# Splitting the next group's rows earlier, and moving two steps of the recurrence, in a one-core hybrid layer

## Chip, cores and metric

The kernel runs on one core of a Trainium2 chip. The metric is device time in microseconds (us); less is better. One compiled program computes the whole layer, and its inputs and outputs lie in HBM.

## What is computed

A layer of a streaming encoder over 2048 positions of width 1024, float32 throughout. The parts that the change touches, cut from the reference:

```python
h = rms_norm(x, mix_norm_g[i])
z = h @ w_in[i]                        # 1024 -> 3328 columns
y_conv = short_conv_mixer(z_conv, conv_mix_w[i])       # B * conv3(C * x_in)
y_rwkv = rwkv7_mixer(z_rwkv, ...)      # g = sigmoid(gd) @ g_up ; o = wkv7_scan(...) ; o * g
x = x + concatenate([y_conv, y_rwkv], axis=-1) @ w_out[i]
x = x + conv_glu_ffn(rms_norm(x, ffn_norm_g[i]), ...)  # 1024 -> 5632 -> 1024
e = rms_norm(p[i] @ ple_w_proj[i], ple_norm_g[i])
gate = sigmoid(rms_norm(x, ple_gate_norm_g[i]) @ ple_w_gate[i])
x = x + gate * e
return rms_norm(x, final_norm_g)
```

wkv7_scan is a recurrence over positions in 8 heads of 64. The kernel does it in chunks of 64 positions, with a triangular solve in each chunk.

## The kernel before

Positions are cut into 4 groups of 512. Activations lie transposed, 128 channels by 512 positions in a tile, which is called a row here (8 rows for width 1024). A float32 product is made of three faster ones: each operand is split into a high part in the float32r type (hi) and a remainder (lo), and `mm3` issues hi*hi, hi*lo and lo*hi. Weights are split in the first group that uses them (ScalarE copy, GpSimd subtraction, line 154), written to HBM as split pairs (SP's queue, line 175) and read from there by the later groups (GpSimd's queue, line 165). The ring of weight halves has four places, that is two products.

**Two streams share TensorE.** The dense stream is a generator. First `all_in` runs the input projection of all four groups, 26 products each. Then, for each group, `dense_rest` runs the output projection (8 products), the up and down projections of the feed-forward part, a small embedding product, and the gate product (8 products). A product is 24 matmuls of 128x128 by 512; it yields in the middle and at its end. The side stream `rwkv` is the recurrence: 16 units of 128 positions, each a generator of 41 steps. `drive` takes a step of the side stream for each step of the dense one (0.85 of a step in the output and gate projections). The side stream begins in the second half of the first input group, and ends in the third group's gate projection. `rest(n)` lets n steps pass; R_LM, R_LOAD, R_DN and so on are such counts.

**Order on the engines.** Each engine runs its instructions in one fixed order. Matmuls keep the order in which they are written, and so do instructions marked with `pin`. All others are placed by a planner that simulates the program before it is compiled; `high_priority` moves them ahead.

**Rows.** `Rows.add` squares a row for the norm (`SumSq.add`: ScalarE L233, VectorE add L237) and splits it with its gain (`split_g`: ScalarE L218, VectorE L221). The norm's factor is applied behind the product: the first two products of a projection are held (HELD = 2) until the sum of squares is complete. Rows y, the input of the output projection, are the mixers' outputs; they come from HBM, have no norm, and are split by `residual` (ScalarE copy L155, pinned; GpSimd subtraction L158). Rows 0 to 3 of y are written by the short convolution during the input projection, rows 4 to 7 by the units of the recurrence. `in_next(g)` and `out_next(g)` load row k and split row k - 1 at call k. Loads share a ring of four buffers, the split halves a ring of 32, which is two sets of eight rows.

**A unit of the recurrence**, as far as it matters here: step 1 ps_s, ps_a; step 2 ps_n, ps_v; step 3 ps_l twice, then ps_g (the gate-lora product) and its copy. Later the score products and the matrix lt, which goes through HBM (ld on ScalarE's queue, lm on SP's) and comes back in another layout. R_LM steps later `fold` starts the triangular solve on VectorE: three instructions and 16 pairs of a multiply (L828) and a reduction (L832). The result goes through HBM again (xd, dt on SP's queue); the next unit's rows are loaded behind it. R_LOAD steps later `rwkv_first` prepares the next unit; R_DN steps later `dn` transposes dt, pinned on VectorE; the rest of the 20 steps (WAIT) pass, and the products gm_ps and x_ps use dn. Seven of these PSUM tiles a unit, and eight others, come from one pool of three buffers.

Of the kernel before, what the change touches and what calls it, by code (L numbers as in the profile page):

```python
# [9 lines left out]
F32 = mybir.dt.float32  # L10
# [6 lines left out]
P = 128  # L17
G = 512
KD = 8
# [1 line left out]
PLE_AT = 2  # L21
HELD = 2
WAIT = 20
R_LM = 4
R_DN = 7
R_POST = 3
R_LOAD = 6
# [37 lines left out]
def tile_trunk(  # L65
# [18 lines left out]
    nc = tc.nc  # L84
    T = xT.shape[2]

    def matmul(*args, **kw):
        return pin(nc.tensor.matmul(*args, **kw))  # L88
# [4 lines left out]
    def pin(ins):  # L93
        return tc.keep_in_program_order(ins)

    NG = T // G
# [25 lines left out]
    def v(name, i, n=1):  # L122
        o, _ = VEC[name]
        return vec[:, o + i : o + i + n]
# [56 lines left out]
    def weight(pools, src, name):  # L181
        return [
            half(pools, src[:, 512 * c : 512 * c + 512], f"{name}_{c}", f"{name}_{c}")
            for c in range(2)
        ]
# [13 lines left out]
    def blk(k):  # L199
        return slice(k * P, (k + 1) * P)  # L200

    def buf(pools, name):
        return pools["tmp"].tile([P, G], F32, tag="b", name=name, bufs=NBUF)
# [6 lines left out]
    def slot(pools, name):  # L210
        return pools["act"].tile([P, G], F32R, tag="act", name=name)

    def pair(pools):
        return slot(pools, "hi"), slot(pools, "lo")

    def split_g(pools, src, gcol, dst, late=False):
        hi, lo = dst
        ins = nc.scalar.activation(hi, src, AF.Copy, scale=gcol)  # L218
        if late:
            pin(ins)  # L220
        nc.vector.scalar_tensor_tensor(  # L221
            out=lo, in0=src, scalar=gcol, in1=hi.bitcast(F32), op0=ALU.mult, op1=ALU.subtract
        )
        return dst
# [43 lines left out]
    class Rows:  # L268
# [1 line left out]
            self.hs, self.ss, self.scale, self.held = [], SumSq(), None, []  # L270

        def add(self, pools, x, gcol, late=False):
            self.ss.add(pools, x, late)
            with tc.high_priority():
                self.hs.append(split_g(pools, x, gcol, pair(pools), late))

    def product(pools, w, rows, evac):
        ps = pools["psd"].tile([P, G], F32, tag="d", name="ps_mm")
# [26 lines left out]
    def in_proj(pools, g, rows, nxt):  # L305
        def project(m, evac):
            return product(pools, weight(pools, w_in[m], f"in{m}"), rows, evac)

        def lerp(j):
            def evac(ps, rstd):  # L310
                zb = scaled(pools, ps, rstd, z_last[:, j : j + 1], 1)
                u = buf(pools, "u")
                nc.scalar.activation(u, zb[:, 2 : G + 2], AF.Copy, scale=mu_c[:, j : j + 1])
                nc.vector.scalar_tensor_tensor(
                    out=u, in0=zb[:, 1 : G + 1], scalar=v("rwkv_mu", j), in1=u,
                    op0=ALU.mult, op1=ALU.add,
                )
                nc.scalar.dma_start(out=zs[g][:, j, :], in_=u)
            return evac

        for j in (12, 0, 4, 8, 13, 1, 5, 9, 2, 6, 10, 3, 7, 11):
            yield from project(12 + j, lerp(j))

        for i in range(4):
            st = {}

            def evac_x(ps, rstd):
                x = st["x"] = buf(pools, "xin")
                nc.vector.tensor_tensor(out=x, in0=ps, in1=rstd, op=ALU.mult)
                nc.vector.tensor_tensor(out=x, in0=x, in1=rstd, op=ALU.mult)  # L330

            def evac_c(ps, rstd):
                t = scaled(pools, ps, st["x"], cx_last[:, i, :], 2)
                u = st["c"] = buf(pools, "cu")
                nc.scalar.activation(u, t[:, 2 : G + 2], AF.Copy, scale=v("conv_mix_w", 8 + i))
                for d in (1, 0):
                    nc.vector.scalar_tensor_tensor(
                        out=u, in0=t[:, d : d + G], scalar=v("conv_mix_w", 4 * d + i), in1=u,
                        op0=ALU.mult, op1=ALU.add,
                    )  # L340

            def evac_b(ps, rstd):
                u = buf(pools, "yc")
                nc.vector.tensor_tensor(out=u, in0=ps, in1=rstd, op=ALU.mult)
                nc.vector.tensor_tensor(out=u, in0=u, in1=st["c"], op=ALU.mult)
                nc.scalar.dma_start(out=ys[g][:, i, :], in_=u)

            if i:
                nxt(3 * i - 3)
            yield from project(i, evac_x)  # L350
            if i:
                nxt(3 * i - 2)
            yield from project(8 + i, evac_c)
            if i:
                nxt(3 * i - 1)
            yield from project(4 + i, evac_b)

    def ple_load(pools, g):
# [44 lines left out]
    def dense_rest(pools, g, yrows, nxt):  # L403
# [3 lines left out]
        rows = Rows()  # L407
# [94 lines left out]
        def e_load(m):  # L502
            with tc.high_priority():
                return staged(pools, es[g][:, m, :], "e")

        ahead = e_load(0)
        for m in range(KD):
            nxt(m)
            w = weight(pools, w_gate[m], f"g{m}")
            e = ahead  # L510
            with tc.high_priority():
                nc.vector.tensor_tensor(out=e, in0=e, in1=re, op=ALU.mult)

            def evac(ps, rstd, m=m, e=e):
                th = buf(pools, "gt")
                nc.vector.tensor_tensor(out=th, in0=ps, in1=rstd, op=ALU.mult)
                if m:
                    ss.add(pools, x2[m - 1])
                nc.scalar.activation(th, th, AF.Tanh, scale=0.5)
                nc.vector.scalar_tensor_tensor(  # L520
                    out=th, in0=th, scalar=1.0, in1=e, op0=ALU.add, op1=ALU.mult
                )
                nc.vector.scalar_tensor_tensor(
                    out=x2[m], in0=th, scalar=pg_h[:, m : m + 1], in1=x2[m],
                    op0=ALU.mult, op1=ALU.add,
                )
                if m == KD - 1:
                    ss.add(pools, x2[m])

            steps = product(pools, w, rows3, evac)  # L530
            next(steps)
            yield SLOW
            if m + 1 < KD:
                ahead = e_load(m + 1)
            for _ in steps:
                yield SLOW
        nxt(KD)

        def finish():
            rstd = ss.rstd(pools)  # L540
# [69 lines left out]
    def rwkv_unit(rp, S, u, loaded, following):  # L610
        pr, ch, ps_p, ps_c = rp["prep"], rp["chain"], rp["ps_p"], rp["ps_c"]
        g, off = u // 4, (u % 4) * P
# [3 lines left out]
        def big(name, tag="t", pool=rp["t"]):  # L616
            return pool.tile([P, 4, P], F32, tag=tag, name=f"{name}{u}")
# [23 lines left out]
        r_t, k_t, v_t, gd, kr, sq = loaded  # L641
# [8 lines left out]
            matmul(ps[:, ct, :], S["aup"][:, blk(ct)], ad, start=True, stop=True)  # L650
        tha = big("tha")
        nc.scalar.activation(tha, ps, AF.Tanh, scale=0.5)
        yield

        ps_n = ps_p.tile([P, G], F32, tag="p", name="ps_n")
# [42 lines left out]
        for cp in range(2):  # L698
            ps = ps_p.tile([P, G], F32, tag="p", name="ps_l")
            for c in range(2):  # L700
                matmul(
                    ps[:, c * 130 : c * 130 + 130], sg[:, blk(2 * cp + c)], tri[:, 0:130],
                    start=True, stop=True,
# [1 line left out]
            pv = ps[:, 0:260].rearrange("p (a c i) -> p a c i", a=2, c=2)  # L705
            nc.scalar.activation(ep[:, 2 * cp : 2 * cp + 2], pv, AF.Exp, scale=-DECAY)
            nc.scalar.activation(em[:, 2 * cp : 2 * cp + 2], pv, AF.Exp, scale=DECAY)
        ps_g = ps_p.tile([P, 4, P], F32, tag="p", name="ps_g")
        for ct in range(4):
            matmul(ps_g[:, ct, :], S["gup"][:, blk(ct)], gd, start=True, stop=True)  # L710
        g_t = big("g")
        nc.scalar.copy(g_t, ps_g)
        yield
        yield

# [90 lines left out]
        for r in range(4):  # L806
# [4 lines left out]
            )  # L811
        yield from rest(R_LM)
        lmf = lm.rearrange("p i j -> p (i j)")
# [48 lines left out]
        for pq in range(4):  # L862
            q = pq % 2
            rs = slice(32 * pq, 32 * pq + 32)
            pin(nc.gpsimd.tensor_copy(tT[rs, :, :, 32 * q : 32 * q + 32], dt4[rs]))
        yield from rest(WAIT - R_LM - R_LOAD - R_DN)
        gm_ps = ps_c.tile([P, 8, 32], F32, tag="c", name="gm_ps")
        for n in range(8):
            c, ct = n // 4, n % 4
# [101 lines left out]
    pools, rp = {}, {}  # L971
# [13 lines left out]
    S = rwkv_setup(rp)  # L985
# [13 lines left out]
    rows = {(kind, g): Rows() for kind in ("in", "out") for g in range(NG)}  # L999
# [2 lines left out]

    def in_next(g):
        def run(k):
            if g < NG:
                if k < KD:
                    loads["in", g, k] = in_load(pools, g, k)
                if k:
                    in_row(pools, rows["in", g], k - 1, loads.pop(("in", g, k - 1)), g > 0)
        return run  # L1010

    def out_next(g):
        def run(k):
            if g < NG:
                if k < KD:
                    while k >= 4 and marks["done"] < 4 * g + 3:
                        next(side, None)
                    loads["out", g, k] = out_load(pools, g, k)
                if k:
                    out_row(pools, rows["out", g], k - 1, loads.pop(("out", g, k - 1)))  # L1020
        return run
# [10 lines left out]

    def all_in():
        for g in range(NG):
            yield from in_proj(pools, g, rows["in", g], in_next(g + 1))

    for k in range(KD + 1):
        in_next(0)(k)
# [7 lines left out]
            ):  # L1046
                tc.keep_in_program_order(nc.scalar.dma_start(out=dst, in_=src))
    drive(stream)
    for k in range(KD + 1):
        out_next(0)(k)  # L1050
    for g in range(NG):
        drive(dense_rest(pools, g, rows["out", g], out_next(g + 1)))
# [69 lines left out]
```

## Time and profile before

| | |
|---|---|
| median of 3 runs | 2913.43 us (2905.58 to 2913.78) |
| profiled execution | 2908.33 us, span of the instructions 2906.6 us |
| mean granted TensorE clock | 0.981 of full speed |
| TensorE (PE) busy | 2767.7 us, 95% |
| VectorE (DVE) busy | 1921.2 us, 66% |
| GpSimd (POOL) busy | 1106.0 us, 38% |
| ScalarE (ACT) busy | 961.6 us, 33% |
| HBM traffic | 216 GB/s over the span |

PE is TensorE's matmuls, PEld its weight loads, which overlap them; SP is the engine that issues DMAs. The profiled execution is one run of its own; its span is the time from the first to the last instruction. A line number (L88) is the line in the kernel; helpers that issue for many callers have one line, so the tile's name tells the instructions apart (ps_mm is a product's sum, whlo the split weights of the output projection, whlu, whld and whlg those of up, down and gate). An arrow points from what an instruction waits for to what it writes: `hi<-y` writes hi from y.

### The profile page before, as it was taken

How to read it: one execution, taken by the hardware profiler on the slowest of the kernel's cores; microseconds unless marked ns; L12 is line 12 of the kernel's file. 1: busy time of each engine (PE TensorE's matmuls, PEld its weight loads, DVE VectorE, ACT ScalarE, POOL GpSimd, SP SyncE). 2: the span in 40 equal slices, each digit the busy share in tenths (PEclk: the TensorE clock that was granted, in tenths of full speed). 3: DMA queues.
4: the chain of work that ended last, by engine and by line, in shares of the span. 5: the costliest groups of instructions: out<-in, count | busy, mean ns of one | idle time of the engine just before them, and what ended most of it. 6: DMA issues, size and time to landing. Idle time of an engine off the chain costs nothing.

```text
span 2906.6 us, 42088 instructions
## 1 busy us (share of the span) xinstructions
PE 2767.7 (95%) x15464; PEld 2228.2 (77%) x15464; DVE 1921.2 (66%) x3039; ACT 961.6 (33%) x1721; POOL 1106.0 (38%) x1700
## 2 busy tenths in 40 slices
PE   8989999998999999889999999899999999999997
PEld 6778778886777867667778887678788877788885
DVE  4575656646788777786876677777676865544446
ACT  4432231313453334343512123434122233411114
POOL 4532232324556556452433333333333332433321
PEclk9999999999999999999999999999999999999998
DMA  9886767777777767667665665777566668766665
GB/s 321 297 268 205 232 206 227 215 213 231 247 262 261 242 241 248 221 221 241 212 182 170 187 185 167 216 218 215 171 185 179 180 183 261 223 193 191 191 193 166
DMA packets 285801, 629.94 MB, mean 217 GB/s; under 512 B 60186, under 2 KB 113690, under 8 KB 285596
## 3 DMA queue, kind: packets, MB, share of 16 engines
q0 software_dynamic: 95040, 346.07, 39.7%
q1 hardware_dynamic: 144384, 238.08, 24.6%
q10 hardware_dynamic: 46172, 43.11, 4.5%
q8 instruction: 122, 2.00, 0.3%
q14 instruction: 83, 0.68, 0.1%
HBM read 467.77 MB, written 159.38 MB: 216 GB/s over the span
## 4 chain that ended last, share of the span: by engine, by line
PE 60%; DVE 19%; DMA 8%; issue 7%; ACT 3%; POOL 2%; SPq 1%; ACTq 0%; DVEq 0%; POOLq 0%
PE ps_mm L88 40%; PE ps_d L88 12%; DVE uf L433 3%; DVE pd L828 2%; PE ps_e L88 2%; DVE xs L832 1%; DMA lm<-ld 1%; PE o_ps L88 1%; DVE zb L263 1%; DMA whlo<-ko 1%; DMA ld<-ltt 1%; DMA whld<-kd 1%; PE s_ps L88 1%; PE u_ps L88 1%; DVE sq L237 1%
## 5 line engine op out<-in xcount | busy, mean ns | idle before, releaser
L88 PE MATMUL ps_mm<-hi,whlu 128*128 128x512 f32 x2816 | 905.5, 396 | 3.4 <-POOL whlu L158 2.3
L88 PEld LDWEIGHTS ps_mm<-hi,whlu 128*128 128x128 f32 x2816 | 531.1, 189 | 119.8 <-POOL whlu L158 3.9
L88 PE MATMUL ps_mm<-hi,whlin 128*128 128x512 f32 x1664 | 540.6, 399 | 16.9 <-DVE xs L832 8.1
L88 PE MATMUL ps_mm<-lo,whlu 128*128 128x512 f32 x1408 | 550.7, 391 | 0.4 <-DVE lo L221 0.4
L88 PE MATMUL ps_d<-hi,whld 128*128 128x512 f32 x1408 | 462.6, 401 | 20.6 <-DVE x L473 8.3
L88 PEld LDWEIGHTS ps_mm<-hi,whlin 128*128 128x128 f32 x1664 | 316.3, 190 | 88.0 <-DVE xs L832 8.9
L433 DVE SCALAR_TENSOR_TENSOR uf<-zb,vec,uf 128x512 f32<-128x512 f32 x352 | 305.7, 870 | 108.8 <-ACT uf L428 97.5
L88 PEld LDWEIGHTS ps_d<-hi,whld 128*128 128x128 f32 x1408 | 269.4, 192 | 85.6 <-DVE x L473 11.2
L88 PE MATMUL ps_mm<-lo,whlin 128*128 128x512 f32 x832 | 328.5, 395 | 2.4 <-DVE lo L221 2.4
L88 PEld LDWEIGHTS ps_mm<-lo,whlu 128*128 128x128 f32 x1408 | 266.2, 189 | 55.8 <-issue 1.9
L428 ACT ACTIVATE uf<-zb,vec 128x512 f32<-128x512 f32 x176 | 143.1, 815 | 493.5 <-DVE zb L263 491.9
L165 POOL DMA_DIRECT2D whlu<-ku x264 | 142.2, 539 | 426.1 <-PE ps_mm L88 281.6
L263 DVE TENSOR_TENSOR zb<-ps_mm,rstd 128x512 f32<-128x512 f32 x216 | 148.6, 688 | 207.1 <-PE ps_mm L88 204.8
L88 PE MATMUL ps_d<-lo,whld 128*128 128x512 f32 x704 | 278.5, 396 | 0.0
L473 DVE TENSOR_TENSOR x<-ps_d,x 128x512 f32<-128x512 f32 x192 | 131.1, 686 | 144.5 <-PE ps_d L88 144.2
L165 POOL DMA_DIRECT2D whlin<-kin x156 | 84.2, 540 | 277.5 <-PE ps_mm L88 243.5
L88 PE MATMUL ps_mm<-hi,whlo 128*128 128x512 f32 x512 | 169.9, 408 | 20.0 <-ACT hi L155 18.2
L88 PEld LDWEIGHTS ps_mm<-lo,whlin 128*128 128x128 f32 x832 | 158.2, 190 | 37.5 <-DVE lo L221 6.2
L88 PE MATMUL ps_mm<-hi,whlg 128*128 128x512 f32 x512 | 166.3, 399 | 2.0 <-DMA whlg<-kg 2.0
L233 ACT ACTIVATE sq<-x 128x512 f32<-128x512 f32 x128 | 80.6, 630 | 255.4 <-DVE x L411 73.6
L158 POOL TENSOR_TENSOR lo<-th,hi 128x512 fp32r<-128x512 f32 x88 | 117.0, 1330 | 113.8 <-ACT hi L155 113.6
L88 PEld LDWEIGHTS ps_d<-lo,whld 128*128 128x128 f32 x704 | 135.2, 192 | 26.7
(205 smaller groups left out, 4266.9 us busy)
## 6 DMA issues: line engine op xcount, KB each, us to landing
whlu<-ku POOLq DMA_DIRECT2D x264, 512.0 KB, 4.4
whlin<-kin POOLq DMA_DIRECT2D x156, 512.0 KB, 4.6
whld<-kd POOLq DMA_DIRECT2D x132, 512.0 KB, 4.1
ku<-whlu SPq DMA_DIRECT2D x88, 512.0 KB, 4.7
kin<-whlin SPq DMA_DIRECT2D x52, 512.0 KB, 5.3
whlo<-ko POOLq DMA_DIRECT2D x48, 512.0 KB, 6.1
whlg<-kg POOLq DMA_DIRECT2D x48, 512.0 KB, 3.8
rawu<-in_w_up SPq DMA_DIRECT2D x88, 256.0 KB, 4.0
```

Source lines behind the costliest of these rows:

```text
L88: return pin(nc.tensor.matmul(*args, **kw))
L158: nc.gpsimd.tensor_tensor(out=lo, in0=raw, in1=hi.bitcast(F32), op=ALU.subtract)
L165: nc.gpsimd.dma_start(out=t, in_=kept[key])
L233: ins = nc.scalar.activation(sq, x, AF.Square)
L237: nc.vector.tensor_tensor(out=sq, in0=sq, in1=self.acc, op=ALU.add)
L263: nc.vector.tensor_tensor(out=zb[:, 2 : G + 2], in0=ps, in1=rstd, op=ALU.mult)
L428: nc.scalar.activation(u, zb[:, 2 : G + 2], AF.Identity, bias=v("ffn_conv_b", n), scale=v("ffn_conv_w", 88 + n),)
L433: nc.vector.scalar_tensor_tensor(out=u, in0=zb[:, d : d + G], scalar=v("ffn_conv_w", 44 * d + n), in1=u, op0=ALU.mult, op1=ALU.add,)
L473: nc.vector.tensor_tensor(out=x2[m], in0=ps, in1=x2[m], op=ALU.add)
L828: tt(out=pd[:, :, :, 0:n], in0=xs[:, :, None, 0:n].broadcast_to([P, 8, 2, n]), in1=lm[:, None, i : i + 2, 0:n].broadcast_to([P, 8, 2, n]), ...
L832: nc.vector.tensor_reduce(out=xs[:, :, i : i + 2], in_=pd[:, :, :, 0:n], op=ALU.add, axis=mybir.AxisListType.X,)
```

## The change

Five edits:

1. The input groups' `nxt` calls come two products sooner: calls 0 to 8 stand ahead of products 15 to 23 of 26, where they stood ahead of 17 to 25. In the last input group, which has no next one, the calls are those of the first output projection instead, up to call 3: four loads of y rows, three splits.
2. In the gate projection call 0 stands ahead of the first load of e, and call m + 1 ahead of product m; before, call m stood there, and call 8 behind the last product.
3. `Rows.add` splits a row first, and squares it then.
4. The gate-lora product and its copy are written in the unit's first step instead of the third.
5. R_LM is 5 instead of 4. The sum of the steps up to gm_ps stays 20, so that the last rest ahead of gm_ps is 2 steps instead of 3.

```diff
@@ -21,7 +21,7 @@
 PLE_AT = 2
 HELD = 2
 WAIT = 20
-R_LM = 4
+R_LM = 5
 R_DN = 7
 R_POST = 3
 R_LOAD = 6
@@ -270,9 +270,9 @@
             self.hs, self.ss, self.scale, self.held = [], SumSq(), None, []
 
         def add(self, pools, x, gcol, late=False):
-            self.ss.add(pools, x, late)
             with tc.high_priority():
                 self.hs.append(split_g(pools, x, gcol, pair(pools), late))
+            self.ss.add(pools, x, late)
 
     def product(pools, w, rows, evac):
         ps = pools["psd"].tile([P, G], F32, tag="d", name="ps_mm")
@@ -345,14 +345,11 @@
                 nc.vector.tensor_tensor(out=u, in0=u, in1=st["c"], op=ALU.mult)
                 nc.scalar.dma_start(out=ys[g][:, i, :], in_=u)
 
-            if i:
-                nxt(3 * i - 3)
+            nxt(3 * i - 1)
             yield from project(i, evac_x)
-            if i:
-                nxt(3 * i - 2)
+            nxt(3 * i)
             yield from project(8 + i, evac_c)
-            if i:
-                nxt(3 * i - 1)
+            nxt(3 * i + 1)
             yield from project(4 + i, evac_b)
 
     def ple_load(pools, g):
@@ -503,9 +500,10 @@
             with tc.high_priority():
                 return staged(pools, es[g][:, m, :], "e")
 
+        nxt(0)
         ahead = e_load(0)
         for m in range(KD):
-            nxt(m)
+            nxt(m + 1)
             w = weight(pools, w_gate[m], f"g{m}")
             e = ahead
             with tc.high_priority():
@@ -534,7 +532,6 @@
                 ahead = e_load(m + 1)
             for _ in steps:
                 yield SLOW
-        nxt(KD)
 
         def finish():
             rstd = ss.rstd(pools)
@@ -650,6 +647,11 @@
             matmul(ps[:, ct, :], S["aup"][:, blk(ct)], ad, start=True, stop=True)
         tha = big("tha")
         nc.scalar.activation(tha, ps, AF.Tanh, scale=0.5)
+        ps_g = ps_p.tile([P, 4, P], F32, tag="p", name="ps_g")
+        for ct in range(4):
+            matmul(ps_g[:, ct, :], S["gup"][:, blk(ct)], gd, start=True, stop=True)
+        g_t = big("g")
+        nc.scalar.copy(g_t, ps_g)
         yield
 
         ps_n = ps_p.tile([P, G], F32, tag="p", name="ps_n")
@@ -705,11 +707,6 @@
             pv = ps[:, 0:260].rearrange("p (a c i) -> p a c i", a=2, c=2)
             nc.scalar.activation(ep[:, 2 * cp : 2 * cp + 2], pv, AF.Exp, scale=-DECAY)
             nc.scalar.activation(em[:, 2 * cp : 2 * cp + 2], pv, AF.Exp, scale=DECAY)
-        ps_g = ps_p.tile([P, 4, P], F32, tag="p", name="ps_g")
-        for ct in range(4):
-            matmul(ps_g[:, ct, :], S["gup"][:, blk(ct)], gd, start=True, stop=True)
-        g_t = big("g")
-        nc.scalar.copy(g_t, ps_g)
         yield
         yield
 
@@ -1002,16 +999,16 @@
 
     def in_next(g):
         def run(k):
-            if g < NG:
+            if 0 <= k <= KD and g < NG:
                 if k < KD:
                     loads["in", g, k] = in_load(pools, g, k)
                 if k:
                     in_row(pools, rows["in", g], k - 1, loads.pop(("in", g, k - 1)), g > 0)
         return run
 
-    def out_next(g):
+    def out_next(g, upto=KD):
         def run(k):
-            if g < NG:
+            if 0 <= k <= upto and g < NG:
                 if k < KD:
                     while k >= 4 and marks["done"] < 4 * g + 3:
                         next(side, None)
@@ -1032,7 +1029,8 @@
 
     def all_in():
         for g in range(NG):
-            yield from in_proj(pools, g, rows["in", g], in_next(g + 1))
+            nxt = in_next(g + 1) if g + 1 < NG else out_next(0, KD // 2 - 1)
+            yield from in_proj(pools, g, rows["in", g], nxt)
 
     for k in range(KD + 1):
         in_next(0)(k)
@@ -1046,7 +1044,7 @@
             ):
                 tc.keep_in_program_order(nc.scalar.dma_start(out=dst, in_=src))
     drive(stream)
-    for k in range(KD + 1):
+    for k in range(KD // 2, KD + 1):
         out_next(0)(k)
     for g in range(NG):
         drive(dense_rest(pools, g, rows["out", g], out_next(g + 1)))
```

## Rows read from the trace of the kernel before

**Rows 1.** The page, part 1: busy us, share of the span, instructions.
```profile
PE 2767.7 (95%) x15464; PEld 2228.2 (77%) x15464; DVE 1921.2 (66%) x3039; ACT 961.6 (33%) x1721; POOL 1106.0 (38%) x1700
```

**Rows 2.** TensorE's waits: waiter and releaser; us in total, times, longest.
```profile
PE ps_mm L88 <- ACT hi L155: 18.2, 5, 4.9
PE ps_d L88 <- DVE x L473: 8.3, 5, 3.6
...
PE ps_g L88 <- ACT em L707: 6.8, 3, 2.8
...
PE ps_mm L88 <- DVE lo L221: 3.3, 6, 1.0
PE ps_g L88 <- DVE suv L688: 3.2, 4, 1.1
```

**Rows 3.** The chain that ended last: start us, us, what.
```profile
2569.67 43.52 PE ps_mm L88 x192
```

**Rows 4.** Timeline, TensorE, at the four boundaries: start, us, instruction, [idle before <-releaser].
```profile
694.19 0.79 PE L88 MATMUL ps_mm<-hi,whlo 128*128 128x512 f32 x1 [4.23 <-ACT hi L155]
...
1315.91 0.80 PE L88 MATMUL ps_mm<-hi,whlo 128*128 128x512 f32 x1 [4.57 <-ACT hi L155]
...
1876.64 0.80 PE L88 MATMUL ps_mm<-hi,whlo 128*128 128x512 f32 x1 [4.95 <-ACT hi L155]
...
2421.41 0.50 PE L88 MATMUL ps_mm<-hi,whlo 128*128 128x512 f32 x1 [2.88 <-ACT hi L155]
...
2423.76 0.77 PE L88 MATMUL ps_mm<-hi,whlo 128*128 128x512 f32 x1 [0.28 <-DMA whlo<-ko]
```

**Rows 5.** Timeline, VectorE: the first output product's evacuation.
```profile
709.08 0.69 DVE L411 TENSOR_TENSOR x<-ps_mm,xr 128x512 f32<-128x512 f32 x1 [17.19 <-PE ps_mm L88]
```

**Rows 6.** Stretches: length, busy us of each engine, TensorE clock, DMA share, GB/s.
```profile
1315.90:1321.20 5.30, 4.74 (x10) 3.43 (x11) 1.55 (x3) 1.25 (x2) 1.83 (x2) 0.50 0.53 134
...
2039.20:2044.80 5.60, 5.59 (x13) 4.43 (x14) 4.97 (x16) 0.00 (x0) 1.24 (x4) 0.50 0.61 186
...
1201.80:1208.60 6.80, 6.54 (x45) 5.32 (x46) 0.80 (x3) 0.73 (x2) 2.50 (x2) 0.50 0.74 257
...
690.00:1311.00 621.00, 567.67 (x3259) 451.75 (x3259) 475.22 (x667) 270.85 (x499) 354.45 (x345) 0.96 0.72 244
```

**Rows 7.** Timeline, GpSimd, at the first boundary.
```profile
694.37 4.97 POOL L158 TENSOR_TENSOR lo<-y,hi 128x512 fp32r<-128x512 f32 x4
```

**Rows 8.** Timeline, ScalarE, at the second boundary.
```profile
1303.32 0.60 ACT L155 CAST hi<-y 128x512 fp32r<-128x512 f32 x1
...
1315.26 0.60 ACT L155 CAST hi<-y 128x512 fp32r<-128x512 f32 x1
```

**Rows 9.** Timeline, GpSimd, at the fourth boundary.
```profile
2416.81 1.63 POOL L165 DMA_DIRECT2D whlo<-ko  x3
```

**Rows 10.** Groups by line: count | busy us, mean ns | idle before, releasers.
```profile
L233 ACT ACTIVATE sq<-x 128x512 f32<-128x512 f32 x128 | 80.6, 630 | 255.4 <-DVE x L411 73.6 <-DVE x L523 64.7 <-DVE x L473 58.1
```

**Rows 11.** Timeline, VectorE, while GpSimd subtracts.
```profile
1280.83 1.78 DVE L743 TENSOR_TENSOR km<-tha,k 128x512 f32<-128x512 f32 x1
```

**Rows 12.** Timeline, VectorE: five of the sixteen folds.
```profile
1008.40 1.77 DVE L817 TENSOR_TENSOR fold<-lm,c_sq 128x512 f32<-128x512 f32 x1
...
1152.01 0.69 DVE L817 TENSOR_TENSOR fold<-lm,c_sq 128x512 f32<-128x512 f32 x1 [0.67 <-issue]
...
1734.39 1.43 DVE L817 TENSOR_TENSOR fold<-lm,c_sq 128x512 f32<-128x512 f32 x1 [1.15 <-DMA lm<-ld]
...
1903.02 0.68 DVE L817 TENSOR_TENSOR fold<-lm,c_sq 128x512 f32<-128x512 f32 x1
...
2037.14 0.69 DVE L817 TENSOR_TENSOR fold<-lm,c_sq 128x512 f32<-128x512 f32 x1 [6.99 <-DMA lm<-ld]
```

**Rows 13.** dn (L858): VectorE's idle before it, and who waited for it.
```profile
  DMA dt<-xd: 45.5, 12
...
  PEld gm_ps L88: 8.4, 5
```

## The prediction, made before the changed kernel ran

> **What bounds the kernel now.** I read the page first: TensorE is busy for 2767.7 of 2906.6 us, every other engine for two thirds of the span or less [rows 1]. So the kernel is bound by the order of its matmuls, and a change can win only what TensorE idles, 139 us, and what its clock loses after an idle stretch. No arithmetic is removed. The second view is TensorE's list of waits, the third its timeline around the longest of them, the fourth a table of stretches with the granted clock; then the queues that were named as releasers. The list says which idle time this change can touch at all [rows 2]: 18.2 us for a copy of a y row (ACT L155), 6.8 and 3.2 us at the gate-lora product (ps_g), 8.3 us at the down product for an evacuation on VectorE, 3.3 us for a split row (L221). The unit of time is the half product, one step of the dense stream: 192 matmuls took 43.52 us [rows 3], 0.227 us each, so 12 take 2.72 and a product of 24 takes 5.44 us.
>
> **Part 1, y rows ahead of the output projection.** Four times a projection starts on rows that are not split [rows 4].
>
> First boundary: idle begins at 694.19 - 4.23 = 689.96 and the first product is picked up at 709.08 [rows 5], 19.1 us for 5.44 us of matmuls, 13.7 too many. What a lower clock cost in that stretch is inside the 13.7. The rows go through GpSimd one by one: four subtractions from 694.37 took 4.97 us, 1.24 each [rows 7]. Now three of the eight rows are split inside the last input group (three loads, copies and subtractions move there, past SP's weight loads), and the buffers that they free let three more loads start early. Three subtractions fewer are 3.7 us, the lower bound; all is 13.7. I take 6: row 7 still needs the buffer of row 3, so its load, copy and subtraction stay behind the boundary.
>
> Second and third: 4.57 and 4.95 us idle, in front of the last of eight rows. That row's copy stands at 1315.26 on ScalarE; the copy of the row before it ran at 1303.32 [rows 8]. The change puts row 7 where row 6 stood, 8 us ahead of the idle's begin at 1311.3. So the idle goes, and with it the slow matmuls behind: 4.74 us busy at a granted clock of 0.50, the 1.2 GHz level of the two (1.2 and 2.4), cost 2.4 [rows 6]. I take 7.0 for the second and the same for the third, 14 together, nothing below (rival A).
>
> Fourth: 2.88 us idle at 2421.41. Here I ask what is late next: 0.28 us at 2423.76 was a wait for the second product's weights [rows 4], whose loads GpSimd issued from 2416.81 on [rows 9]. Nothing in the change issues them sooner. Product 0 would end some 4 us earlier, and wait for those weights. I take 0, bound 4.
>
> **Part 2, x rows two products sooner.** No row of the list of waits names an x row behind the first group, so nothing is gained. Each row moves a load, two ScalarE and two VectorE instructions by 11 us, into the same stage; TensorE covers them. Cost 0; if the cover failed, a row would cost its 0.63 us square at most [rows 10], 15 us over 24 rows.
>
> At this place the Trainium skill speaks against the change: GPSIMD Engine Reference, Key points, says that GpSimd shares its SBUF interfaces with VectorE, and that instructions with two SBUF inputs contend. The trace agrees: a VectorE multiply beside a GpSimd subtraction took 1.78 us [rows 11], against 0.69 us of the same form [rows 12]. By the rule, the three subtractions moved into the input stage stretch up to three VectorE instructions by 1.1 us, 3.3 us if none were hidden.
>
> **Part 3, split ahead of squaring.** A row's two halves leave ScalarE 0.63 us sooner [rows 10], and the running sum leaves that much later; that sum is wanted two products on, 10.9 us, so it costs 0. Split rows were waited for 3.3 us in six places [rows 2]; one square each is the most that goes, but the square of the row before still stands ahead. I take 1, bounds 0 and 3.3.
>
> **Part 4, gate-lora product in the first step.** Its eight matmuls and one copy stay; only their place moves, by two steps. In the old place it waited 6.8 + 3.2 = 10.0 us for a PSUM buffer whose readers (exponentials, subtractions) had just been issued [rows 2]. In the new place its operand has been ready since rwkv_first, some 20 steps before, and the buffer is that of an earlier product. A wait of the second ps_l for a reduction, ahead of it, stays. I take 8; bounds 0 (the wait moves to the next product) and 10.
>
> **Part 5, one more step ahead of fold.** fold is pinned on VectorE and waits for four loads: at 2037.14 the engine sat 6.99 us [rows 12], with the evacuations of two down products queued behind it, and TensorE waited for these: 8.3 us in five places [rows 2]. One step is 2.72 us; it lets the next evacuation pass. TensorE's longest such wait, 3.6, falls to 0.9. Of the 8.3 I take 6, and of the slow matmuls behind (5.59 us busy at 0.50, 2.8 us lost [rows 6]) all: 9. Bounds 5 and 11.
>
> With fold move its 32 solve instructions, the store and the four loads on SP, the next unit's six loads, ps_b and rwkv_first. The step comes out of the wait ahead of gm_ps, so dn has one step less. Behind gm_ps on TensorE stand all products. Five units of sixteen already have weight loads of gm_ps waiting for dn [rows 13]. What a unit loses is the step less the idle time that fold had: 2.72 at 1008.40 and at 1903.02 (no idle), 2.05 at 1152.01, 1.57 at 1734.39 [rows 12]; where fold idled a step or longer, 0. Sum 9.1 if all of these had no slack, 0 if all had it. As dn waits for its loads in 12 units [rows 13], I take the whole 9.
>
> **Sum.** 6 + 14 + 0 + 0 + 1 + 8 + 9 - 9 = 29 us. Against the profiled execution's own 2908.33 that is 2879. It ran 5.1 us under the median of the runs, 2913.43; half of that brings me to 2882. All gains at their bounds, with no loss at dn, would be 13.7 + 14 + 4 + 3.3 + 10 + 11 = 56 (2855); all at the low ones, with the loss, 3.7 + 5 - 9 = 0. What a measurement can tell from no change is about 0.3%, 9 us.
>
> **Rivals.**
>
> A. The y rows land no sooner. The last y copy is late because loads, buffers and ScalarE's queue are, not because of its place: at 1315.26 it stood behind a square and the issue of four stores. Then the 14 us stay and the gain is 15: 2896. Against it: row 6's copy ran 12 us before row 7's [rows 8], with nothing special about it. The Trainium skill, DMA: Bandwidth & Descriptors, Issuing engines are not separate DMA queues, says that all queues interleave on the same 16 engines; a load issued sooner into a full stretch then lands little sooner. No row here shows one row's landing both ways.
>
> B. The waits come back. In the stage from 690 to 1311 us VectorE is busy 475 of 621 us [rows 6], in program order; a wait that goes at ps_g returns as a late evacuation, and dn takes the rest. If parts 1 and 5 give half (10 + 4.5) and part 4 nothing, less 9, 6 us remain: 2905, within 0.3%.
>
> C. The solve comes too late (slower). If a full step is lost at gm_ps in most units, each costs 2.72, and the clock behind: in a stretch from 1201.8, behind such a wait, 6.54 us were busy at 0.50 [rows 6], 3.3 lost. At 6.0 a unit it decides from eight units on (48 against the 38 gained). With 12, the units whose dn waits today, it is 72 - 38 = 34 slower: 2945. For it: 45.5 us of VectorE's idle time at dn [rows 13]. Against it: in eleven units gm_ps does not wait for dn at all.
>
> **Chances.** My forecast (a gain of 17 to 50) 0.60, more than that 0.02, rival A 0.13, B 0.15, C 0.10. Faster by over 0.3% are the first three, 0.75; same 0.15; slower 0.10. The range, 2858 to 2908, takes in A, half of B, and all but the best of the gains; C and the other half of B are left out, near 2 in 10. The likeliest case alone spans 2860 to 2894.
>
> **What would show it.** No wait of TensorE for a y copy at the second and third boundary, and a clock of 1.0 behind; the fourth with a wait for weights in its place; the first with its product picked up some 13 us after the idle's begin, not 19. No wait at ps_g. fold's idle time down by 2.7 a unit, evacuations ahead of it. gm_ps with more waits, some 15 us in all. The forecast is wrong if gm_ps waits for over 30 us, if the y copies still end TensorE's longest waits, or if ps_g waits for a buffer in its new place.

## The result: 0.6% slower

The changed kernel takes 2926.87 us (median of 6 runs, 2921.7 to 2933.44) against 2912.86 for the kernel before on the same chip: a ratio of 1.0059, 95% interval 1.0043 to 1.0075, or 12.5 to 22 us slower. The forecast was 2882. The profiled execution has a span of 2919.9 us, 13.3 more than before, and a granted clock of 0.978 (before 0.981).

**The profile after.** Part 1 of the page, which answers to [rows 1]:

```profile
PE 2766.2 (95%) x15464; PEld 2231.9 (76%) x15464; DVE 1905.6 (65%) x3039; ACT 963.7 (33%) x1721; POOL 1109.5 (38%) x1700
```

TensorE is as busy as before (2767.7), so the loss is idle time: span less busy time is 153.7 us where it was 138.9. TensorE's list of waits, for [rows 2] (behind the input projection most of this kernel's line numbers are 2 or 3 lower):

```profile
PE gm_ps L88 <- DVE dn L855: 35.8, 10, 5.5
PE ps_d L88 <- DVE x L470: 11.2, 8, 2.8
PE ps_d L88 <- ACT hi L155: 9.2, 2, 8.3
...
PE ps_mm L88 <- DVE lo L221: 5.6, 5, 2.3
...
PE ps_mm L88 <- DMA whlo<-ko: 4.4, 3, 3.0
...
PE ps_mm L88 <- ACT hi L155: 2.8, 2, 2.5
```

The wait for y copies is nearly gone (18.2 to 2.8), the one at ps_g wholly (10.0 to nothing: no row has it). Two rows are new at the top. gm_ps waits 35.8 us in ten units for dn, and the down product waits 8.3 us once for a row th whose copy (hi, L155) is late. The kernel before had for gm_ps:

```profile
PE gm_ps L88 <- DVE dn L858: 6.3, 3, 3.2
```

TensorE's timeline, for [rows 4], with two of the new waits between the boundaries:

```profile
689.90 0.64 PE L88 MATMUL ps_mm<-hi,whlo 128*128 128x512 f32 x1 [2.47 <-ACT hi L155]
...
1128.48 0.76 PE L88 MATMUL ps_d<-hi,whld 128*128 128x512 f32 x1 [8.29 <-ACT hi L155]
...
1382.63 1.06 PE L88 MATMUL gm_ps<-dn,lt 32*32 32x32 f32 x32 [5.54 <-DVE dn L855]
...
2439.21 0.47 PE L88 MATMUL ps_mm<-hi,whlo 128*128 128x512 f32 x1 [3.02 <-DMA whlo<-ko]
```

At the second and third boundary no y copy is waited for (the granted clock behind them is 1.00 from 1312.90 to 1318.20, and 0.74 from 1878.40 to 1884.00); at the fourth the weights are. VectorE's timeline, for [rows 5], and two dn:

```profile
698.81 0.69 DVE L408 TENSOR_TENSOR x<-ps_mm,xr 128x512 f32<-128x512 f32 x1 [11.49 <-PE ps_mm L88]
...
1053.91 0.44 DVE L855 STREAM_TRANSPOSE dn<-dt 128x256 f32<-128x256 f32 x1 [5.82 <-DMA dt<-xd]
...
1382.15 0.43 DVE L855 STREAM_TRANSPOSE dn<-dt 128x256 f32<-128x256 f32 x1
```

The first output product is picked up 11.4 us after the idle's begin (698.81 less 689.90 - 2.47), where it took 19.1. The two dn are late in two ways. The one at 1053.91 waited 5.82 us for its data. The one at 1382.15 waited for nothing: VectorE was busy up to it, and it stands late in VectorE's order. What dn as a whole waited for and held up, for [rows 13]; then fold's idle time, in the kernel before and in this one:

```profile
  DMA dt<-xd: 33.2, 9
...
  PEld gm_ps L88: 40.0, 10
```

```profile
  DMA lm<-ld: 33.6, 11
```

```profile
  DMA lm<-ld: 13.9, 5
```

VectorE's own wait for the loads ahead of fold fell, 33.6 to 13.9 us, as the fifth step was to do. The clock behind a wait at gm_ps, for [rows 6] (length, busy of PE, PEld, DVE, ACT, POOL, clock, DMA share, GB/s):

```profile
1382.60:1386.40 3.80, 3.77 (x39) 3.12 (x40) 3.26 (x5) 2.17 (x4) 1.65 (x4) 0.50 0.33 107
```

3.77 us at the 1.2 GHz level are 1.9 lost on top of the 5.54 idle. Last, a row of VectorE's list of waits, of which the kernel before has none:

```profile
DVE b L725 <- DMA ys<-yt: 34.8, 11, 6.4
```

### The profile page after: what moved, and what is told of

It reads as the page before. It is cut to its first block, busy times and chain, and to the rows that moved or that the text cites. A ratio compares the mean times of both kernels' runs of the same rounds, so it can differ in the third digit from the quotient of the medians.

```text
span 2919.9 us, 42057 instructions
## 1 busy us (share of the span) xinstructions
PE 2766.2 (95%) x15464; PEld 2231.9 (76%) x15464; DVE 1905.6 (65%) x3039; ACT 963.7 (33%) x1721; POOL 1109.5 (38%) x1700
## 5 line engine op out<-in xcount | busy, mean ns | idle before, releaser
L430 DVE SCALAR_TENSOR_TENSOR uf<-zb,vec,uf 128x512 f32<-128x512 f32 x352 | 297.6, 848 | 108.6 <-ACT uf L425 98.6
L158 POOL TENSOR_TENSOR whlu<-rawu,whlu 128x512 fp32r<-128x512 f32 x88 | 125.3, 1427 | 84.0 <-ACT whlu L155 76.8
```

What stands on the lines that cost most here:

```text
L158: nc.gpsimd.tensor_tensor(out=lo, in0=raw, in1=hi.bitcast(F32), op=ALU.subtract)
L430: nc.vector.scalar_tensor_tensor(out=u, in0=zb[:, d : d + G], scalar=v("ffn_conv_w", 44 * d + n), in1=u, op0=ALU.mult, op1=ALU.add,)
```

## Experiments

The theory after this profile: R_LM = 5 takes from the answer of the solve a step that most units do not have (the rival C of the prediction), and the gate-lora move puts work late on VectorE in the first dense stage (rival B). Against it: the waits at gm_ps could be harmless, no more than the place where time gained elsewhere is waited out, and another part the loss. Ratios are to the kernel before, with 95% intervals.

### The step ahead of fold

**The changed kernel with R_LM = 4.**

```diff
-R_LM = 5
+R_LM = 4
```

> The changed kernel with R_LM back at 4; all its other edits stay. Theory 1 (the step taken from the wait ahead of gm_ps costs the 29.5 us by which TensorE's waits at gm_ps grew, and some 8 us of clock behind them): about 2885 to 2895 us, waits at gm_ps back to some 6 to 12 us. Theory 2 (the moved rows and the moved gate-lora product put VectorE's order out of step, R_LM is innocent): 2920 to 2930, no change that can be measured against the changed kernel.

2912.69 us, ratio 1.0 [0.9986, 1.0014]: between the two theories. The wait at gm_ps goes as theory 1 says, and with it 17 us by ratio; but the time is that of the kernel before, 18 us or more over theory 1, so that among the other edits something loses what others gain. The row:

```profile
PE gm_ps L88 <- DVE dn L855: 7.8, 4, 3.1
```

**The kernel before with R_LM = 5 alone** (the opposite edit).

> The kernel before with R_LM = 5 and no other edit. Theory 1: slower than before by 15 to 35 us, 2928 to 2948, with 30 us or more of waits at gm_ps. Theory 2: within 9 us of before, and faster if the 8.3 us of down-product waits behind fold go.

2929.38 us, 1.006 [1.004, 1.008]: alone it costs as much as the whole change.

```profile
PE gm_ps L88 <- DVE dn L858: 38.1, 10, 5.5
```

By the page TensorE idles 159.1 us here (span 2929.8, busy 2770.7), 20.2 more than before. The wait at gm_ps grew by 31.8, so all other idle time fell by 11.6. Of that, the row that the step was to shorten (8.3 us in [rows 2]) gives 2.3:

```profile
PE ps_d L88 <- DVE x L473: 6.0, 6, 2.2
```

In the kernel before, TensorE's timeline has two of that row's five waits behind a fold; the other three stand amid the solve or behind bk:

```profile
1477.42 0.50 PE L88 MATMUL ps_d<-hi,whld 128*128 128x512 f32 x1 [3.04 <-DVE x L473]
...
2039.21 0.79 PE L88 MATMUL ps_d<-hi,whld 128*128 128x512 f32 x1 [3.57 <-DVE x L473]
```

With R_LM = 5 the first is 2.17 us (at 1492.59) and the second is gone, 4.4 us less; two short ones amid a solve are new. No slow matmuls are saved: TensorE is busy 3.0 us longer. The rest of the 11.6 lies in rows that do not wait for fold, and may be no more than time now waited out at gm_ps; no run tells. So the gain in its own place was about half of the 9 forecast, and the wait at gm_ps grew by three and a half times the 9 forecast for the loss.

**The answer one step later.** The changed kernel, with the step taken from the end of the unit instead.

```diff
-WAIT = 20
+WAIT = 21
-R_POST = 3
+R_POST = 2
```

> The changed kernel with WAIT = 21 and R_POST = 2: gm_ps one step later, so that its distance from fold is what it was before, the unit still 41 steps. Theory 1: the waits at gm_ps fall from 35.8 to under 12 us and the time to 2885 to 2897, while fold keeps its later place and its idle time stays near 14 us. Theory 2: 2920 or more. If the last rest of the unit, shortened by a step, matters, new waits show at ps_y.

2902.92 us, 0.9967 [0.9953, 0.9981]: by ratio 27 us faster than the changed kernel, and 6 us above the range of theory 1.

```profile
PE ps_y L91 <- DVE on L620: 15.2, 9, 3.0
PE gm_ps L88 <- DVE dn L855: 11.0, 6, 2.8
```

The step is now missing ahead of ps_y, in nine units and by less (2.3 us in two units in the changed kernel).

**dn one step sooner.** The changed kernel, gm_ps at its place.

```diff
-R_DN = 7
+R_DN = 6
```

> The changed kernel with R_DN = 6: dn back at its old distance from gm_ps, the solve still a step later. If dn's own place in VectorE's order is what is late (three units waited for gm_ps with dt long landed: 2.8, 5.5 and 5.5 us), those 14 us go and VectorE idles longer at dn: 2905 to 2915. If the landing of dt is what is late, as in the other seven units (22 us), nothing is gained: 2922 to 2932.

2912.78 us, 1.0005 [0.9992, 1.0018], by ratio 16 us faster than the changed kernel.

```profile
PE gm_ps L88 <- DVE dn L855: 21.1, 7, 4.7
```

14.7 us of waits go. Most of it is dn's own place on VectorE: the three units that waited for dn with its data long landed (2.82, 5.54 and 5.54 us in the changed kernel, the second of them at 1382.63) wait 0, 1.24 and 0.64 us here. All that still wait, wait for the data, as at 1053.91.

**The changed kernel with R_LM = 3.**

```diff
-R_LM = 5
+R_LM = 3
```

> The changed kernel with R_LM = 3, so that the solve stands two steps sooner than in it. Theory 1 has a price on both sides: waits at gm_ps near 0, but fold idles for its loads in nearly all units (more than 33 us), with evacuations queued behind it. About 2890 to 2905, near R_LM = 4. Theory 2: 2920 or more.

2924.6 us, 1.0049 [1.0033, 1.0064], where theory 1 has 2890 to 2905. One step less than R_LM = 4 costs about as much as one more. The wait at gm_ps is small (4.3 us, once) and fold idles 55.1 us for its loads (over 33 forecast). More evacuations of down products are late (10.2 us with R_LM = 4), and still more the weights of the output projection (3.6 with R_LM = 4), which no theory here named:

```profile
PE ps_d L88 <- DVE x L470: 16.0, 11, 3.8
PE ps_mm L88 <- DMA whlo<-ko: 12.9, 6, 6.7
```

### The gate-lora move

**The move alone**, in the kernel before.

```diff
         nc.scalar.activation(tha, ps, AF.Tanh, scale=0.5)
+        ps_g = ps_p.tile([P, 4, P], F32, tag="p", name="ps_g")
...
+        nc.scalar.copy(g_t, ps_g)
         yield
```

> The kernel before with the gate-lora product and its copy in the unit's first step, and no other edit. By the prediction: 10 us of waits at ps_g go, 8 us faster, 2905. Rival (the waits come back on VectorE, whose exponentials and score operands follow): within 3 us of before, with ps_g at 0 and other waits in its place.

2920.34 us, 1.004 [1.0027, 1.0053]: 11.6 us slower, where a gain of 8 was forecast. No wait at ps_g is left. In its place, in TensorE's list, and then the longest in its timeline:

```profile
PE ps_d L88 <- DVE x L473: 11.6, 6, 4.1
PE ps_d L88 <- ACT hi L155: 9.6, 2, 8.3
```

```profile
1138.87 0.77 PE L88 MATMUL ps_d<-hi,whld 128*128 128x512 f32 x1 [8.35 <-ACT hi L155]
```

It follows from VectorE's order. First the kernel before, VectorE's timeline at the same place, then this one:

```profile
1118.28 0.68 DVE L449 TENSOR_TENSOR th<-th,uf 128x512 f32<-128x512 f32 x1
1118.88 0.68 DVE L728 SCALAR_TENSOR_TENSOR b<-tha,kr 128x512 f32<-128x512 f32 x1
```

```profile
1118.06 0.69 DVE L728 SCALAR_TENSOR_TENSOR b<-tha,kr 128x512 f32<-128x512 f32 x1 [4.40 <-DMA ys<-yt]
...
1135.71 1.69 DVE L746 TENSOR_TENSOR bk<-km,em 64x512 f32<-64x512 f32 x1
...
1137.43 0.69 DVE L449 TENSOR_TENSOR th<-th,uf 128x512 f32<-128x512 f32 x1
```

Before, th, which the next down product needs, stands ahead of b and of the four products bk behind it. With the move, the planner places b, km and bk sooner, ahead of th (why it does so is not shown). And b asks for a buffer of pool t (nine buffers) that yt of the last unit holds until its store has landed, 4.40 us later. It is no other buffer than before: in the trace of the kernel before b waits on that store's semaphore too, but comes so late that the store has landed (issued at 1105.80, at most 6.3 us to landing, b at 1118.88). So the new order does two things: b waits for the store with all of VectorE behind it, and th stands behind bk.

**The move alone, with yt in another buffer** (lm's, free at that time).

```diff
-        yt = big("yt")
+        yt = ch.tile([P, 4, P], F32, tag="lm", name=f"yt{u}", bufs=1)
```

> Kernel before with only the gate-lora move, as in the run of that move alone (2920.3 us, ratio 1.004), but yt no longer takes a buffer of the nine-buffer pool t: it takes the buffer of lm, which holds nothing between the end of one unit's solve and the load of the next unit's lm. Theory 1, the move loses time because b now asks for its buffer about 4.5 us before the store of the last unit's yt out of that buffer has landed, and VectorE's work queues behind b: the waits of b for ys<-yt (36.8 us, 12 of them in the run of the move alone) go to nothing, the wait of ps_d for ACT hi near 1130 us (8.3 us) goes, the first dense stage comes back from 630 to about 615 us, and the time is 2900 to 2908 us, ratio 0.995 to 0.998, a little under before since the ps_g wait (10 us) is gone too. Theory 2, VectorE's new order (b, km and the rest ahead of th) is the cause, whoever holds the buffer: the waits of b go, but hi is as late as before, the stage keeps about 628 us, and the time is 2916 to 2922 us, ratio 1.002 to 1.004.

2914.97 us, 1.0018 [1.0006, 1.0029]: between the two theories. b waits for no store any more, and half of the loss goes (yt elsewhere also leaves one more place in pool t to other tiles, which is not told apart). The wait for hi stays, since th still stands behind bk; TensorE's list, and VectorE's timeline:

```profile
PE ps_d L88 <- ACT hi L155: 8.8, 2, 7.4
```

```profile
1122.72 1.68 DVE L746 TENSOR_TENSOR bk<-km,em 64x512 f32<-64x512 f32 x1
1124.44 0.69 DVE L449 TENSOR_TENSOR th<-th,uf 128x512 f32<-128x512 f32 x1
```

**The move alone, with b held in program order on VectorE.**

```diff
-        nc.vector.scalar_tensor_tensor(
+        pin(nc.vector.scalar_tensor_tensor(
             out=b_t, in0=tha, scalar=1.0, in1=kr, op0=ALU.add, op1=ALU.mult
-        )
+        ))
```

> Kernel before with only the gate-lora move, and b held in the order in which the program gives it on VectorE, so that it stands again behind suv and the first two products of ari, and km behind bk. TensorE's order is that of the move alone (2920.3 us, ratio 1.004). Theory 1, the loss is VectorE's new order: no wait of b for ys<-yt, no wait of ps_d for ACT hi near 1130 us (8.3 us), first dense stage at about 612 to 617 us, and with the ps_g waits (10 us) gone as well 2898 to 2908 us, ratio 0.994 to 0.998. Theory 2, the loss is in the moved matmuls and the copy themselves (ps_s, ps_a and ps_g share three banks and ScalarE in one step): 2914 to 2922 us, ratio 1.001 to 1.004.

2915.78 us, 1.0008 [0.9994, 1.0022]: the loss is gone, and theory 1 is right about that; the gain it foresaw did not come. The first dense stage, by windows of the kernel before, the move alone, yt elsewhere, and b held:

```profile
694.20:1306.40 612.20, 563.05 (x3238) 447.98 (x3239) 468.96 (x656) 268.92 (x496) 352.33 (x343) 0.96 0.72 244
```

```profile
692.70:1323.00 630.30, 571.79 (x3239) 453.83 (x3240) 468.31 (x658) 268.65 (x497) 349.69 (x343) 0.94 0.70 239
```

```profile
692.60:1309.40 616.80, 563.84 (x3239) 447.15 (x3240) 470.14 (x657) 268.88 (x496) 350.41 (x342) 0.95 0.72 244
```

```profile
699.10:1312.60 613.50, 564.28 (x3238) 448.99 (x3239) 473.97 (x656) 267.89 (x496) 351.90 (x343) 0.96 0.72 244
```

18 us more with the move, of which 8.7 are slower matmuls (571.79 less 563.05); 4.6 more with yt elsewhere, 1.3 with the order mended. So the order was the cause of the loss in this stage; outside it the kernel with the move alone is 6 us shorter than before. With b held, in place of the 10 us of ps_g TensorE's list has 9.3 us more at the unit's next products, which wait for bk. The kernel before, then b held:

```profile
PE ps_o L88 <- DVE bk L746: 1.3, 1, 1.3
...
PE ps_e L88 <- DVE bk L745: 1.0, 1, 1.0
```

```profile
PE ps_e L88 <- DVE bk L745: 7.8, 5, 4.5
...
PE ps_o L88 <- DVE bk L746: 3.8, 5, 1.2
```

### Rows and split

**The split ahead of squaring alone** (edit 3 in the kernel before).

> The kernel before with rows split ahead of squaring, and no other edit. By the prediction 1 us, which can't be measured: 2904 to 2922. If the later squares hold the norm's factor back, the third product's buffer waits and it is slower by over 9 us.

2904.29 us, 0.998 [0.9964, 0.9995]. The wait for split rows, which the edit was to shorten, did not fall (3.3 us in [rows 2]):

```profile
PE ps_mm L88 <- DVE lo L221: 5.6, 6, 2.2
```

**The rows sooner alone** (edits 1 and 2).

> The kernel before with the rows' calls moved sooner (input groups by two products, gate projections by one, three y rows in the last input group), and no other edit. By the prediction 6 + 14 us: 2893, with no wait for y copies at the second and third boundary and a wait for weights at the fourth. Rival (the rows' VectorE and GpSimd work in the gate projection delays its evacuations and the unit there): 2905 to 2915.

2902.57 us, 0.9978 [0.9964, 0.9993]. The y copies go, and weights come in their place (1.8 us for whlo before, and no row for whlin):

```profile
PE ps_mm L88 <- DMA whlin<-kin: 10.3, 4, 5.9
PE ps_mm L88 <- DMA whlo<-ko: 9.9, 5, 3.5
...
PE ps_mm L88 <- ACT hi L155: 3.5, 2, 2.3
```

Not all of the weights' waits are new. The longest stood in the kernel before at the same matmul, put down to another releaser. TensorE's timeline, before and here:

```profile
182.76 0.77 PE L88 MATMUL ps_mm<-hi,whlin 128*128 128x512 f32 x1 [6.98 <-DVE xs L832]
```

```profile
182.19 0.77 PE L88 MATMUL ps_mm<-hi,whlin 128*128 128x512 f32 x1 [5.86 <-DMA whlin<-kin]
```

**Both together**, edits 1 to 3.

> Changed kernel without the gate-lora move and with R_LM = 4: the rows sooner and the split ahead of squaring, together. Alone they measured 2902.6 (ratio 0.9978) and 2904.3 (0.998). If they are independent, the sum is 0.9958, about 2900 us. If the rows' gain is eaten by the weight loads (whlin, whlo late, 20 us of waits in the rows' run alone), the split adds nothing or takes part away: 2902 to 2908 us. If the loss of the changed kernel came out of these two together, and not out of R_LM = 5 and the gate-lora move: over 2912 us.

2903.65 us, 0.9975 [0.996, 0.999]: no more than either alone.

### Versions

**Edits 1, 2, 3 and 5, with the later answer** (WAIT = 21, R_POST = 2), without the gate-lora move.

> Changed kernel without the gate-lora move, with R_LM = 5, and the solve's answer one step later (WAIT = 21, R_POST = 2). The one run of the changed kernel with the later answer came to 2902.9 us, with the gate-lora move in it. If that move's loss (10 us alone) is independent of the fold's step: 2893 us, ratio 0.993, first dense stage about 615 us. If the step given to the fold is worth nothing but the one taken from the end of the unit costs (ps_y waited 15 us there): 2898 to 2904 us, as or above the run of rows and split together.

2899.33 us, 0.9964 [0.9951, 0.9977], the lowest ratio of all.

```profile
PE ps_y L91 <- DVE on L620: 14.5, 9, 3.0
PE gm_ps L88 <- DVE dn L855: 12.6, 7, 2.8
...
PE ps_d L88 <- DVE x L470: 5.3, 6, 1.8
```

**The changed kernel with R_LM = 4 and yt in lm's buffer.**

> Changed kernel with R_LM = 4 and with yt in the buffer of lm in place of one of pool t: rows sooner, split ahead, gate-lora in the first step, without the two losses named so far. With R_LM = 4 alone it measured 2912.7 us, ratio 1.0. Theory 1 (b waits for the store of yt): the first dense stage goes from 629 to about 614 us, no wait of b for ys<-yt, and the time is 2893 to 2900 us, ratio 0.993 to 0.996. Theory 2 (VectorE's order): about 2910 us, ratio 0.999 to 1.0.

2910.44 us, 1.0 [0.9987, 1.0013]: nothing over R_LM = 4 alone. The order is not mended here, and hi still waits (8.6 us in two places).

**The changed kernel with R_LM = 4 and b held.**

> Changed kernel with R_LM = 4 and b held in program order on VectorE: all the parts that were forecast to gain, without the step ahead of fold. With R_LM = 4 alone it was 2912.7 us, ratio 1.0; rows and split without the gate-lora move were 2903.7 us, ratio 0.9975. Theory 1: about 2896 to 2903 us, ratio 0.994 to 0.9975, the move adding up to 8 us to the gain of the two others or nothing. Theory 2: 2908 to 2914 us, ratio 0.9985 to 1.0.

2906.23 us, 0.9981 [0.9968, 0.9993]: between the theories, and about what rows and split have without the move (0.9975).

**The changed kernel with the later answer and b held.**

> Changed kernel, R_LM = 5, with the answer one step later (WAIT = 21, R_POST = 2) and b held in program order on VectorE. With the later answer alone the changed kernel was 2902.9 us (ratio 0.9967), and without the gate-lora move 2899.3 us (0.9964). Theory 1: the move's loss of 8 to 10 us goes, 2888 to 2896 us, ratio 0.992 to 0.995. Theory 2: 2899 to 2905 us, ratio 0.9955 to 0.997.

2903.41 us, 0.9968 [0.9956, 0.998], as with the later answer alone. So here the held b brings nothing that a measurement can tell, and the move itself costs nothing that one can tell (0.9964 without it).

## Why the prediction was wrong, point by point

The four parts alone, by ratio: rows -6 us, split -6, gate-lora +12, the step +17. The forecast for the same four was -20, -1, -8 and 0. The sum of the four is +17, which is what the change measured, but part of that is luck, since not all of them can be added: with the later answer the gate-lora move costs nothing that can be told (0.9967 with it, 0.9964 without), where alone it costs 12. Rows and split together gain 7 where their sum is 12, and the move costs 7 on top of these two; both differences lie within the intervals. The step costs 17 alone and on top of all the others.

**Part 5, the step: the loss was sized at 9 and is about 30.** The step that failed is "What a unit loses is the step less the idle time that fold had", with 0 for the eleven units that did not wait at gm_ps. Matched unit by unit in the two traces, the wait at gm_ps grew by 4.4, 5.5 and 4.2 us in three of the four units that the text counted, fell by 1.0 in the fourth, and grew in six others, for which the text had 0, by 5.5, 4.1, 2.8, 1.6, 1.2 and 1.2: 29.5 us in all, 16.4 of them in those six. Where a unit waits, it is 3.6 us on average (35.8 by 10), more than the 2.72 of the step, with 1.9 us of slow matmuls behind in the stretch shown.

Two things were left out. dn has a place of its own in VectorE's order: with one step less between dn and gm_ps, three units wait for dn although its data has landed (13.9 us, and 1.9 with dn one step sooner). Two of these three had more than a step to spare before. And the time from fold to dn is not fixed: in the last unit it is 36.6 us before (2296.61 to 2333.16) and 41.7 here (2310.55 to 2352.21), so that a unit with 4.8 us to spare ends with 4.06 of waiting. Why it is longer there isn't settled. The text saw VectorE's wait ahead of dn [rows 13] and took it for rival C, at 0.10. C's mechanism decided, with 10 units where it asked for eight or more, and at a lower price than its 6.0 us a unit; and the text's own sign of being wrong, over 30 us at gm_ps, came.

The gain was sized too high as well. The text read all 8.3 us of late evacuations as waits behind fold; two of the five were, 6.6 us. These fell by 4.4 with R_LM = 5 alone, the whole row by 2.3, and the 2.8 us of slow matmuls did not go.

**Part 4, gate-lora: the sign was wrong.** "In the new place its operand has been ready" holds, and the wait at ps_g went. The step failed in asking only what the moved product waits for, and not what its old place held back: with the product gone from there, the planner moved b, km and bk ahead of th, and b to a time when the store out of its buffer was still under way. Rival B had this form, a wait that "returns as a late evacuation" in that stage, but at no loss; and it took VectorE's order to be the program's, while it is the planner's, which changed. With the order mended, the result is the lower bound of the text: the wait moves to the next products (ps_e and ps_o for bk, 2.3 to 11.6 us).

**Part 1, the y rows: right in every wait, too large in the sum.** Forecast 20, measured 6. The first boundary gave 19.1 - 11.4 = 7.7 us (6 forecast), the second and third lost their waits, and the fourth waits 3.02 us for weights, as said. What failed is that "what is late next" was asked at the fourth boundary alone. In the run of the rows alone 14.7 us of waits for y copies go, and the waits for whlin and whlo grow by 18; 5.9 of these stood in the kernel before under another name, and 12.5 are new: whlo inside the output projections of the second and fourth group above all (2.9 us at 1356.89, 3.5 at 2414.78), and whlin in the input projections. Rival A, that the rows land no sooner, is refuted. The rule of the Trainium skill named there (DMA: Bandwidth & Descriptors, Issuing engines are not separate DMA queues) says that DMAs of all issuing engines run on the same 16 DMA engines and interleave. The traces do not show that the rows' loads slowed those of the weights: from issue to landing a load of whlo took 6.1 us (median) in both kernels, one of whlin 4.6 before and 4.5 with the rows sooner. What they show at 2414.78 is that TensorE came to the weights 12.2 us sooner than in the kernel before, and GpSimd issued their load only 9.0 us sooner (2407.81 against 2416.81): the difference is the wait. For the other waits that isn't worked out. In the changed kernel whlin waits hardly at all (0.2 us), so this is no fixed price.

**Part 2** was run only together with part 1, so that its cost isn't known, nor whether the stretched VectorE instructions that the text feared came. **Part 3** was 1, bounds 0 and 3.3; it measured 6, interval 1.5 to 10, but not by its mechanism: the wait for split rows rose, 3.3 to 5.6 us. Where the 6 us come from isn't settled; together with the rows the edit adds nothing that can be told.

**Still open.** With R_LM = 5 and the later answer the changed kernel is 10 us faster than with R_LM = 4, but the row that the step was to shorten, ps_d waiting for x, is 9.8 us against 10.2; without the gate-lora move the same pair of edits gives 3 us, within the intervals, and that row does fall, 8.3 to 5.3.

## What to carry to other kernels

A step given to one wait of a software pipeline is taken from another: before taking it, read in every unit how long the result lies ready before the later end uses it. Of the seven units that had less than a step to spare here six lost, and of the nine that had more three did, two of them because an instruction in between had its own fixed place. Then try the step at either end (here 3, 4 and 5 have their best at 4, or at 5 with the answer later too). When an operation moves, look in the new static order for what has been let ahead, on every engine it fed, and for which buffer those instructions now ask. Parts of a change that each touch another wait are measured one by one, and together too: two of the four here were gains, and what one of them cost hung on what stood beside it.

## What the runs showed that was not expected

The buffer of yt was free only when the store out of it had landed. In the run of the move alone that store was issued at 1112.73, VectorE's instruction b waited 4.40 us for it, and everything in VectorE's order stood behind b, though b alone asked for that buffer. The Trainium skill (PSUM — Partial Sum Buffer, Engine vs sequencer instructions) calls VectorE's queue strict FIFO, and this row agrees.
